# The out projection of a hybrid encoder block as seven quarter products, with sums of its weights kept in HBM

## The chip, the core and the metric

The kernel runs on one core of a Trainium2 chip. A core has TensorE (PE: matrix products into PSUM), VectorE (DVE), ScalarE (ACT), GpSimd (POOL) and SyncE (SP), which issues most DMAs; all work out of an on-chip memory (SBUF) and PSUM. The metric is the device time of one launch in microseconds (us), lower is better, as the median of several runs.

## The reference

One block over 1024 tokens of 1024 channels, with 16 meta tokens ahead:

```python
h = h + hybrid_mixer(rmsnorm(h, norm_mix), w_in, ..., w_out)
h = h + squared_relu_mlp(rmsnorm(h, norm_ffn), w_ff1, w_ff2)
return rmsnorm(h, norm_final)[:, N_META:]
```

The mixer projects the normed tokens with w_in, makes a pooled branch y_a (trailing means over 2, 4, 8 and 16 positions, a small mix per group, then w_pool_out) and a gated linear attention branch y_b (chunks of 64, then w_gla_out), and merges them:

```python
m = jax.nn.sigmoid(ga) * y_a + jax.nn.sigmoid(gb) * y_b
return jnp.einsum('bld,de->ble', m, w_out)
```

The change is in this last product (1024 x 1024 times 1024 x 1024), called the out projection here, and in what stands directly before and behind it.

## The kernel before

All operands are f32. A product in full precision is made of three: each operand is split into a high part (ScalarE copies it to fp32r) and a low part (VectorE or GpSimd subtracts the copy), and mm3 (L253) issues high x high, high x low and low x high for each 128 x 128 tile of the stationary side and 512 columns of the moving side. So every operand costs a ScalarE copy and a subtraction before TensorE can use it, and 512 columns over a depth of 512 (four tiles) cost 12 matmuls.

The program is one list of steps in the order of TensorE's work, which is written out by hand. Where `in_order` is set for ScalarE and VectorE, these engines take their instructions in the order in which the code issues them; where `any_order` is set, a scheduler places them. GpSimd's order and SyncE's are in the listings below the change. Each engine runs its own list strictly in order: an instruction that waits holds up all that stand behind it on that engine.

The stages, in the order of time: the norm and the projections with w_in; at 240 to 320 us the pooling, where `a_block` projects one group of 128 channels, `mean_block` (L921) makes its trailing means on VectorE, and `mix_block` (L938) multiplies them with w_pool_mix (mw, whose low half is made on GpSimd in L902); the attention; then `yb_block` (L1152), which multiplies the attention's output with w_gla_out, gates it, adds the pooled branch and leaves the merged m, split, in MH (high) and ML (low), one pair for each half of 512 tokens. For the second half of the tokens (h = 1) this runs at about 460 to 488 us.

Out projection before (488.5 to 581 us): `load_wo` (L1518) splits w_out into S["wo"], in pieces of 256 rows by 512 columns; `out_tile(t, ch)` (L1545) multiplies token tile t (128 tokens) with one half ch of the columns: 24 matmuls into one PSUM bank, then VectorE adds the bank to x, which lies in acc (L1559). All eight tiles go with ch = 0 first, then in ORDER with ch = 1. After ch = 1 the row of a tile is complete, and `layer_norm` makes its norm: Square with a running sum on ScalarE (L245), Ln and Exp (L221, L223), four small VectorE instructions, and the scaling (`scaled`, L249) into u2. `turn_tile` (L1567) then transposes the normed tile on TensorE (8 matmuls with the identity, L1577) two tiles later, and makes from it the operands of the first MLP product FF1, which already runs as seven products of sums of quarters: for tiles 0 to 3 the split, and a raw copy of the transposed tile (L1582); for tiles 4 to 7 differences with those raw copies, split into S["wo"][0] (L1599).

Behind that: `ff_weights` (L1642) primes FF1's weights, `ff_room` (L1659) splits one more operand of FF1, called P4 (L1664, L1665), and makes place for h, the hidden values of the MLP. `ff_result` (L1687) forms h, its sums S1, S2, S5, S6, S7, and stores them (`keep`); `ff2_open` (L1713) opens the operands fx of the second MLP product FF2, which reads the stored sums back.

Of the kernel before, what the change touches and what calls it, by code (L numbers as in the profile page):

```python
# [115 lines left out]
def kernel(  # L116
# [52 lines left out]
    pm_dram = dp.tile([2, 2, P, 4, HALF], F32, name="pm_dram")  # L169
    hf_dram = [dp.tile([NPAIR, P, HALF], F32, name=f"hf{m}_dram") for m in range(7)]  # L170
# [66 lines left out]
    def layer_norm(xt, u):  # L237

        scaled(xt, u, inv_rms(xt, u))

    def inv_rms(xt, u):
        rows = xt.shape[0]
        ss = ln_stat[ln_n[0] % 4][:rows]
        ln_n[0] += 1
        act.activation(u, xt, ACT.Square, accum_out=ss)  # L245
        return inv_sqrt(ss, 1, 1.0 / D)

# [21 lines left out]

    def split(a):  # L270

        hi, lo = next_slot()
        if len(a.shape) == 3:
            hi, lo = quad(hi), quad(lo)
        act.activation(hi, a, ACT.Copy)  # L275
        dve.tensor_tensor(lo, a, f32(hi), ALU.subtract)  # L276
        return hi, lo
# [611 lines left out]
    def pool_open():  # L889
# [13 lines left out]
        raw.lend(left.push("raw2", [P, D], F32))  # L903

# [94 lines left out]
    v_ = lambda i: step(one, lambda: load_vw(i))  # L999
    for f, i in (  # L1000
        (a_, 3), (p_, 3), (a_, 2), (m_, 3), (p_, 2), (a_, 1), (m_, 2), (p_, 1), (a_, 0), (m_, 1), (v_, 1), (p_, 0),
    ):
        f(i)
# [127 lines left out]
    def early_gates():  # L1131
# [7 lines left out]
        fetch_wo(0, 0, S["raw3"])  # L1139
# [12 lines left out]
    def yb_block(n, h):  # L1152
        j = YB[h][n]

        def fn(*wbs):
# [6 lines left out]
            for e in range(2):  # L1162
# [20 lines left out]
                if h and e and n == 1:  # L1183
                    load_wo(0, 1)()
                if not h:
                    dve.tensor_tensor(gl, b, gl, ALU.mult)
                dve.tensor_tensor(gl, gl, ml, ALU.add)
# [297 lines left out]
    def merge_open():  # L1485
# [4 lines left out]
        S["wo"] = [left.push("wo0", [P, 2, KT, HALF], F32R)]  # L1490
        S["left_acc"] = left.mark()
        S["acc"] = left.push("acc", [P, 8, D], F32)
# [4 lines left out]
        fetch_wo(0, 1, S["acc"][:, 5])  # L1497
# [8 lines left out]
    fetched = {}  # L1506

    def fetch_wo(ch, kk, at=None):

        c, rows = slice(ch * HALF, (ch + 1) * HALF), w_out[kk * 256 : (kk + 1) * 256]  # L1510
        ap = rows[:, c].rearrange("(k p) c -> p k c", p=P)
        if at is None:
            at = raw.load(ap, D)
        else:
            nc.sync.dma_start(at.rearrange("p (k c) -> p k c", k=2), ap)
        fetched[ch, kk] = at.rearrange("p (k c) -> p k c", k=2)

    def load_wo(ch, kk):  # L1518
        def fn():
            if (ch, kk) not in fetched:  # L1520
                fetch_wo(ch, kk)
            wo, r = S["wo"][ch][:, :, 2 * kk : 2 * kk + 2], fetched.pop((ch, kk))
            act.activation(wo[:, 0], r, ACT.Copy)
            pending.append(lambda: dve.tensor_tensor(wo[:, 1], r, f32(wo[:, 0]), ALU.subtract))
            if ch:
                late()

        return fn

    step(one, merge_open)  # L1530
    def wo1_open():
        any_order("order")
        raw.back()
        right.pop_to(0)
        buffer("u2", 2, D)
        S["u2p"] = right.push("u2p", [P, 2, HALF], F32)
        S["rawx0"] = right.push("rawx0", [P, D], F32)
        raw.lend(S["rawx0"])
        S["right_ff"] = right.mark()
        S["wo"].append(right.push("wo1", [P, 2, KT, HALF], F32R))  # L1540


    ORDER = (0, 4, 1, 5, 2, 3, 6, 7)

    def out_tile(t, ch):  # L1545
        def fn():
            half, at = t // 4, (t % 4) * P
            wo = S["wo"][ch]
            b, n = bank("mm"), ORDER.index(t)
            for j in range(2):  # L1550
                if ch and j and n > 1:
                    turn_tile(ORDER[n - 2])
                mm3(
                    b, KT // 2, lambda i: (MH[half][:, 4 * j + i, at : at + P], ML[half][:, 4 * j + i, at : at + P]),
                    lambda i: (wo[:, 0, 4 * j + i], wo[:, 1, 4 * j + i]), first=j == 0, last=j == 1,
                )
            a = S["acc"][:, t, ch * HALF : (ch + 1) * HALF]
            with tc.high_priority(offset=AHEAD) if ch else nullcontext():
                dve.tensor_tensor(a, b, a, ALU.add)  # L1559
                if ch:  # L1560
                    layer_norm(S["acc"][:, t], S["u2"][:, n % 2])
            if ch:
                nc.sync.dma_start(h_dram[t], S["acc"][:, t])

        return fn

    def turn_tile(t, tags=("ms",), later=None):  # L1567
# [25 lines left out]
        def differences():  # L1593
            dve.tensor_tensor(lo, b[1], t1, ALU.subtract)
            dve.tensor_tensor(b12, b[1], b12, ALU.subtract)
            dve.tensor_tensor(hi, hi, lo, ALU.subtract)
            for n, a in enumerate((lo, b12)):
                fh, fl = (S["wo"][0][:, k, 4 * n : 4 * n + 4, cols] for k in range(2))
                act.activation(fh, a, ACT.Copy)  # L1599
                dve.tensor_tensor(fl, a, f32(fh), ALU.subtract)  # L1600
# [5 lines left out]

    for n, j in enumerate(YB[1]):
        if n != 1:
            step(one, load_wo(0, n))
# [4 lines left out]
        if n < 2:  # L1614
            step(one, lambda kk=n + 2: fetch_wo(0, kk, S["acc"][:, 4 + kk]))
    step(one, load_gB)
    step(one, wo1_open)
    step(one, lambda: x_again(0))
    step(one, lambda: x_again(1))
    for t in range(8):  # L1620
        if t < 6:
# [296 lines left out]
```

## Time and profile before

| | |
|---|---|
| median of 3 runs | 1202.03 us (1201.92 to 1202.49) |
| span of the profiled execution | 1200.9 us, 1.1 below the median of the runs |
| TensorE busy | 1189.0 us, 99%, 6810 matmuls |
| VectorE, ScalarE, GpSimd busy | 873.0, 624.7 and 64.8 us |
| out projection | first matmul at 488.52 us; FF1's first matmul at about 581 |

The profiled execution's own time is taken as its span. Times in rows of the timeline are from the start of the span. A matmul's listed duration runs on beneath the next one, so the distance between starts is what counts. In a group's row the last part is the idle time of that engine just before the instructions, and what ended it. "b_mm", "b_x" and "b_ms" are PSUM banks; "th", "tl" are high and low halves of an operand on the token side, "w1h", "w1l" of a weight.

### The profile page before, as it was taken

Reading aid. Unit: us, or ns where it says so; the run is one execution under the profiler, and the core shown is the slowest. Engines: PE = TensorE matmul, PEld = TensorE weight load, DVE = VectorE, ACT = ScalarE, POOL = GpSimd, SP = SyncE. Lnnn points to the kernel's source line nnn. Section 1 sums busy time; section 2 is a strip of 40 time slices with the busy share of each in tenths; the row PEclk is TensorE's granted clock in tenths of the full one; section 3 lists DMA queues with packets and bytes.
Section 4 is the critical chain, followed back from the end, with each engine's and each line's share of the span. In section 5 each row is a group of like instructions: output and inputs, shape, how many; then the busy total and the mean of one; then the engine's idle time right before and its main releaser. Section 6 shows DMA issues by size and latency. Waiting matters only on the chain.

```text
span 1200.9 us, 18410 instructions
## 1 busy us (share of the span) xinstructions
PE 1189.0 (99%) x6810; PEld 995.0 (83%) x6810; DVE 873.0 (73%) x1436; ACT 624.7 (52%) x1120; POOL 64.8 (5%) x102
## 2 busy tenths in 40 slices
PE   9999999999999999999999999999999999999997
PEld 8888888898998887888888888888888888888885
DVE  7886677666667888637986767767675887887686
ACT  7677567745446433215654545545454444445554
POOL 2200000000103235000000000000000000000000
PEclk9999999999999999999999999999999999999999
DMA  8243433535107676821264444445389963333532
GB/s 259 36 115 116 126 92 99 156 116 161 50 20 265 196 245 196 323 69 77 88 202 132 158 149 160 148 157 164 125 283 332 330 220 97 97 97 97 167 97 88
DMA packets 143722, 183.29 MB, mean 153 GB/s; under 512 B 10328, under 2 KB 80752, under 8 KB 143120
## 3 DMA queue, kind: packets, MB, share of 16 engines
q1 hardware_dynamic: 141648, 176.55, 45.8%
q0 software_dynamic: 1824, 5.31, 1.5%
q8 instruction: 53, 0.87, 0.3%
q14 instruction: 37, 0.30, 0.1%
q10 hardware_dynamic: 160, 0.27, 0.1%
HBM read 124.41 MB, written 57.67 MB: 152 GB/s over the span
## 4 chain that ended last, share of the span: by engine, by line
PE 91%; DVE 3%; DMA 3%; ACT 1%; issue 1%; SPq 0%; POOL 0%; DVEq 0%; ACTq 0%
PE b_mm L257 10%; PE b_mm L259 10%; PE b_mm L258 10%; PE b_ms L259 10%; PE b_ms L258 10%; PE b_ms L257 10%; PE b_x L257 8%; PE b_x L258 8%; PE b_x L259 8%; PE b_sc L1278 1%; PE b_mx L257 1%; DMA ma_dram<-o 1%; PE b_mx L259 1%; PE b_mx L258 1%; DMA o<-ma_dram 1%; DMA t<-gb_dram 1%
## 5 line engine op out<-in xcount | busy, mean ns | idle before, releaser
L257 PE MATMUL b_mm<-th,w1h 128*128 128x512 f32 (+1 forms) x308 | 115.4, 375 | 0.3 <-DVE c L847 0.3
L259 PE MATMUL b_mm<-th,w1l 128*128 128x512 f32 (+1 forms) x308 | 114.2, 371 | 0.0
L258 PE MATMUL b_mm<-tl,w1h 128*128 128x512 f32 (+1 forms) x308 | 114.1, 371 | 0.0
L257 PE MATMUL b_x<-th,w1h 128*128 128x512 f32 (+1 forms) x264 | 100.2, 380 | 0.0
L258 PE MATMUL b_x<-tl,w1h 128*128 128x512 f32 (+1 forms) x264 | 100.1, 379 | 0.0
L259 PE MATMUL b_x<-th,w1l 128*128 128x512 f32 (+1 forms) x264 | 99.7, 378 | 0.0
L275 ACT ACTIVATE w1h<-raw 128x512 fp32r<-128x512 f32 x98 | 60.7, 620 | 27.9 <-PE b_ms L258 13.6
L275 ACT ACTIVATE w1h<-fs 128x512 fp32r<-128x512 f32 x78 | 49.0, 630 | 48.3 <-PE b_ms L258 34.4
L276 DVE TENSOR_TENSOR w1l<-raw,w1h 128x512 fp32r<-128x512 f32 x98 | 67.1, 686 | 8.3 <-ACT w1h L275 8.3
L257 PEld LDWEIGHTS b_mm<-th,w1h 128*128 128x128 f32 x308 | 57.8, 188 | 11.0 <-issue 0.7
L259 PEld LDWEIGHTS b_mm<-th,w1l 128*128 128x128 f32 x308 | 57.8, 188 | 10.1
L258 PEld LDWEIGHTS b_mm<-tl,w1h 128*128 128x128 f32 x308 | 57.9, 188 | 9.6
L276 DVE TENSOR_TENSOR w1l<-fs,w1h 128x512 fp32r<-128x512 f32 x78 | 53.4, 687 | 16.6 <-ACT w1h L275 16.6
L275 ACT ACTIVATE w1h<-bt 128x512 fp32r<-128x512 f32 x44 | 27.8, 632 | 66.8 <-issue 62.7
L259 PEld LDWEIGHTS b_x<-th,w1l 128*128 128x128 f32 x264 | 49.7, 188 | 9.6
L257 PEld LDWEIGHTS b_x<-th,w1h 128*128 128x128 f32 x264 | 49.6, 188 | 9.5
L258 PEld LDWEIGHTS b_x<-tl,w1h 128*128 128x128 f32 x264 | 49.6, 188 | 9.2
L1753 DVE TENSOR_TENSOR bt<-w,w 128x512 f32<-128x512 f32 x80 | 54.8, 685 | 0.6 <-DMA w<-in_w_ff_dram 0.6
L275 ACT ACTIVATE fxh<-bt 128x512 fp32r<-128x512 f32 x36 | 22.8, 632 | 55.7 <-issue 49.8
L275 ACT ACTIVATE w1h<-rawx 128x512 fp32r<-128x512 f32 x44 | 27.4, 628 | 44.6 <-PE b_x L258 18.6
L259 PE MATMUL b_ms<-wo,w1l 128*128 128x512 f32 x128 | 49.9, 390 | 0.0
L257 PE MATMUL b_ms<-wo,w1h 128*128 128x512 f32 x128 | 49.8, 389 | 0.0
(455 smaller groups left out, 3342.3 us busy)
## 6 DMA issues: line engine op xcount, KB each, us to landing
hf_dram<-h SPq DMA_DIRECT2D x112, 256.0 KB, 2.1
raw<-hf_dram SPq DMA_DIRECT2D x112, 256.0 KB, 2.6
w<-in_w_ff_dram SPq DMA_DIRECT2D x64, 256.0 KB, 4.6
raw<-in_w_in_dram SPq DMA_DIRECT2D x22, 512.0 KB, 4.6
raw<-in_w_ff_dram SPq DMA_DIRECT2D x16, 512.0 KB, 4.1
rawx<-in_w_ff_dram SPq DMA_DIRECT2D x16, 512.0 KB, 4.2
rawx<-in_w_in_dram SPq DMA_DIRECT2D x10, 512.0 KB, 4.3
xs<-in_x_dram SPq DMA_DIRECT2D x8, 512.0 KB, 4.9
```

What stands on the lines that cost most here:

```text
L257: pe.matmul(ps, ah, bh, start=first and i == 0, stop=False, skip_group_check=more)
L258: pe.matmul(ps, ah, bl, start=False, stop=False, skip_group_check=more)
L259: pe.matmul(ps, al, bh, start=False, stop=last and i == n - 1, skip_group_check=more)
L275: act.activation(hi, a, ACT.Copy)
L276: dve.tensor_tensor(lo, a, f32(hi), ALU.subtract)
L1278: pe.matmul(b[to, e, j], kk[r, s], qq[r, s], start=True, stop=True, tile_position=(e * CH, u * CH))
L1753: dve.tensor_tensor(bt, w, S["w2"][q[3:]][:, i], ALU.add if q[2] == "+" else ALU.subtract)
```

## The change

With tokens and channels each cut in halves, the projection is a product of 2 x 2 quarters. Instead of eight quarter products it makes seven, of sums of quarters on both sides (P1 and P2, a product with T2, one with T1, and three called third, seventh and fourth by their functions), and adds the results.

- `wo_sums`, on GpSimd during the pooling stage: the four weight sums T1 to T4 are made from w_out's quarters in two halves, and stored to HBM (wt_dram). It is issued behind the first `mean_block`.
- In `yb_block` for the second half of the tokens, the first four channel tiles are no longer split: only their plain sum is kept (in "sums"), and all eight are written there.
- `merge_open` has GpSimd make plain sums of high and low halves of the first token half (`top`); `out_projection` makes from these the token sums (VectorE and GpSimd), splits them into MH and ML, and issues the seven products, one token tile of 12 matmuls at a time.
- The products third, seventh and fourth are interleaved with rows and turns: third(t) completes row t; seventh(t) opens a bank, fourth(t) adds to it and completes row 4 + t. Rows now complete in another order, ORDER = (0, 1, 2, 4, 3, 5, 6, 7).
- The row's norm is made by `first_rms` (one small VectorE instruction less), in two pieces: `row` issues the Square, Ln and Exp, `normed` the smalls and the scaling.
- In `turn_tile` the raw copies and part of the later differences and their low halves go to GpSimd, as do the low halves of FF1's first four weight quarters.
- P4's operand now lies in wx, which is also the place of T4, read by the product fourth. F takes S["wo"][0]'s part. h moves into acc (16 halves) and the first row of u2 (2 halves), which lies where FF2's fx is opened later.

The core of the diff:

```diff
+    def wo_sums():
+        b11, b12, b22, b21 = (S["tsum"][:, n] for n in range(4))
+        for q in range(2):
+            for t, j, k in ((b11, 0, 0), (b12, 0, 1), (b22, 1, 1), (b21, 1, 0)):
+                pool.dma_start(pieces(t), wo_part(j, k, q))
+            for n, (to, a, b) in enumerate(((b11, b12, b11), (b12, b22, b12), (b22, b22, b11), (b21, b21, b22))):
+                pool.tensor_tensor(to, a, b, ALU.subtract)
+                pool.dma_start(wt_dram[n, q], to)
...
-        (a_, 3), (p_, 3), (a_, 2), (m_, 3), (p_, 2), (a_, 1), (m_, 2), (p_, 1), (a_, 0), (m_, 1), (v_, 1), (p_, 0),
+        (a_, 3), (p_, 3), (o_, 0), (a_, 2), (m_, 3), (p_, 2), (a_, 1), (m_, 2), (p_, 1), (a_, 0), (m_, 1), (v_, 1), (p_, 0),
...
+        for t in range(4):
+            b = bank("ms")
+            product(b, form[1, 0], "T1", t)
+            dve.tensor_tensor(w[:, t], b, u[:, t], ALU.add)
+            by_tile(t)
+            add(t, right_of, w[:, t], pool)
+            add(4 + t, right_of, w[:, t], pool)
+            add(4 + t, left_of, u[:, t], pool)
...
+        third(0)
+        sides("T4", 0)
+        normed(0)
+        third(1)
+        rounded("T4", 1, pool)()
+        normed(1)
...
+        seventh(0)
+        turn_tile(0)
+        third(2)
+        turn_tile(1)
+        normed(2)
+        fourth(0)
+        seventh(1)
+        normed(4)
+        turn_tile(2)
+        third(3)
...
+        turn_tile(4, later=later)
+        normed(3)
+        later.pop()()
+        fourth(1)
+        ff_weights()
+        seventh(2)
+        normed(5)
+        turn_tile(3)
+        seventh(3)
+        turn_tile(5, later=later)
+        fourth(2)
+        later.pop()()
+        normed(6)
+        fourth(3)
...
-                act.activation(raw_copy, b[j], ACT.Copy)
-                split_from_psum(MH[0][:, k, cols], ML[0][:, k, cols], b[j])
+                h, l = MH[0][:, k, cols], ML[0][:, k, cols]
+                split_from_psum(h, l, b[j])
+                pool.tensor_tensor(raw_copy, f32(h), f32(l), ALU.add)
...
-        ff_quarters.x["P4"] = tuple(right.push("t4" + k, [P, 4, HALF], F32R) for k in "hl")
+        ff_quarters.x["P4"] = S["wx"][:, 0], S["wx"][:, 1]
...
-        S["h"] = left.push("h", [P, 2, 9, HALF], F32)
+        units = [S["acc"][:, t, c] for t in range(8) for c in halves()] + [S["u2"][:, 0, c] for c in halves()]
+        S["h"] = units[:9], units[9:]
```

How this stands in the engines' lists, at three places. First GpSimd in the pooling stage, before (tl is an operand of the attention that follows; w1l the low half of a weight):

```order
L562 MEMSET lr 80x512
L902 TENSOR_TENSOR mw<-raw_116,mw 128x512
L88 TENSOR_TENSOR w1l<-raw_116,w1h 128x256 x4
L562 MEMSET lr 80x512
L1081 DMA tl_144<-pm_dram 128x2048
```

and after, from the same place (tsum holds the quarters of w_out, then their sums):

```order
L911 DMA tsum<-in_w_out_dram 128x2x512 x4
L913 TENSOR_TENSOR tsum<-tsum 128x1024
L554 MEMSET lr 80x512
L914 DMA wt_dram<-tsum 128x1024
L894 TENSOR_TENSOR mw<-raw_117,mw 128x512
L913 TENSOR_TENSOR tsum<-tsum 128x1024
L914 DMA wt_dram<-tsum 128x1024
```

The split of mw now has four loads, a subtraction and a store in front of it; seven more subtractions and stores follow.

Second, VectorE where the first finished row is normed: before, row 0 (acc is x plus the projection, small the statistics, u_5067 the normed row):

```order
L1559 TENSOR_TENSOR acc<-b_mm,acc 128x512 [waits PE_49]
L222 TENSOR_SCALAR small<-small 128x1 [waits Activation_49]
L225 SCALAR_TENSOR_TENSOR small<-small 128x1 [waits DVE_49,Activation_49]
L229 TENSOR_SCALAR small<-small 128x1 [waits DVE_49]
L230 TENSOR_TENSOR small<-small 128x1 [waits DVE_49]
L249 SCALAR_TENSOR_TENSOR u_5067<-acc,small,gB 128x1024 [waits DVE_49]
```

and after (wx takes T4):

```order
L1632 TENSOR_TENSOR acc<-b_mm,acc 128x512 [waits PE_49,Pool_49]
L1555 TENSOR_TENSOR wx<-raw_117,wx 128x1024 [waits DMAHW2_49,Activation_49]
L623 TENSOR_SCALAR small<-small 128x1
L625 SCALAR_TENSOR_TENSOR small<-small 128x1 [waits DVE_49]
L626 SCALAR_TENSOR_TENSOR small<-small 128x1 [waits DVE_49]
L239 SCALAR_TENSOR_TENSOR u_5117<-acc,small,gB 128x1024 [waits DVE_49]
```

The low half of T4's first part now stands between the addition and the statistics, and waits for ScalarE and a DMA.

Third, ScalarE at row 6, after (wx now takes P4's operand, F the differences of a turn; L618 is the Square, L620 and L621 are Ln and Exp):

```order
L618 ACTIVATE u_5117,small<-acc 128x1024 [waits DMAHW3_49,DVE_49]
L1863 ACTIVATE wx<-acc 128x4x128 [waits PE_49,Pool_49]
L620 ACTIVATE small<-small 128x1 [waits Activation_49]
L1863 ACTIVATE wx<-acc 128x4x128 [waits Pool_49]
L621 ACTIVATE small<-small 128x1 [waits Activation_49]
L1802 ACTIVATE F<-acc 128x4x128 [waits DVE_49] x2
```

Before, the same row had Square, Ln and Exp one behind the other (L245, L221, L223), and P4's copies had a place of their own. Now the first copy into wx, which waits for TensorE and GpSimd, stands between the Square and the logarithm.

More of the change, by code (lines that the diff above doesn't have):

```diff
@@ L1534, in wo1_open, with out_projection @@
+    def out_projection():
         right.pop_to(0)
-        buffer("u2", 2, D)
+        u, w = (left.push("o" + n, [P, 4, HALF], F32) for n in "uw")
         S["u2p"] = right.push("u2p", [P, 2, HALF], F32)
         S["rawx0"] = right.push("rawx0", [P, D], F32)
-        raw.lend(S["rawx0"])
+        S["u2"] = right.push("u2", [P, 2, D], F32)
         S["right_ff"] = right.mark()
[L1540 to L1565, printed above, removed]
@@ new lines, in normed, with third, seventh, fourth @@
+        def normed(t):
+            scaled(acc[:, t], S["u2"][:, ORDER.index(t) % 2], next(rms.pop(t)))
+        def third(t):
+            b = bank("mm")
+            product(b, form[0, 1], "B22", t)
+            add(t, right_of, b)
+            row(t)
+        def seventh(t):
+            b = held[t] = bank("x")
+            product(b, form[1, 0], "T3", t, last=False)
+            add(4 + t, right_of, b)
+        def fourth(t):
+            b = held.pop(t)
+            product(b, form[1, 1], "T4", t, first=False)
+            add(4 + t, left_of, b)
+            row(4 + t)
```

259 lines of the change are left out of this document (192 added, 67 removed).

## The prediction

> **What bounds the kernel now.** I read the page first: the busy shares, the slices, the chain that ended last.
>
> ```profile
> span 1200.9 us, 18410 instructions
> PE 1189.0 (99%) x6810; PEld 995.0 (83%) x6810; DVE 873.0 (73%) x1436; ACT 624.7 (52%) x1120; POOL 64.8 (5%) x102
> POOL 2200000000103235000000000000000000000000
> PE 91%; DVE 3%; DMA 3%; ACT 1%; issue 1%; SPq 0%; POOL 0%; DVEq 0%; ACTq 0%
> ```
>
> TensorE is busy 99% of the span and carries 91% of the chain, so taking matmuls away shortens the kernel as long as no other engine takes over the wait. GpSimd (POOL) is nearly empty and has nothing to do after slice 15, that is after some 480 us. Next I looked at the stretches around the out projection (columns: stretch, its length, then busy us and instructions of PE, PEld, DVE, ACT, POOL, then clock, DMA share, GB/s).
>
> ```profile
> 440.00:475.00 35.00, 34.14 (x236) 27.14 (x235) 27.70 (x44) 13.37 (x22) 24.15 (x28) 1.00 0.65 212
> 475.00:500.00 25.00, 24.95 (x111) 20.34 (x110) 19.57 (x28) 8.38 (x12) 0.00 (x0) 1.00 0.81 273
> 500.00:520.00 20.00, 20.00 (x90) 16.57 (x89) 8.86 (x11) 6.30 (x8) 0.00 (x0) 1.00 0.83 290
> 520.00:540.00 20.00, 20.00 (x90) 16.57 (x89) 3.89 (x7) 1.47 (x4) 0.00 (x0) 1.00 0.03 10
> 540.00:560.00 20.00, 20.00 (x102) 16.80 (x101) 14.23 (x31) 10.85 (x25) 0.00 (x0) 1.00 0.24 96
> 560.00:582.00 22.00, 22.00 (x110) 18.44 (x109) 18.03 (x36) 13.55 (x29) 0.00 (x0) 1.00 0.18 73
> ```
>
> From 500 to 582 TensorE has no gap at the full granted clock (1.00). There is no wait in the projection that the change could remove; all it can win is matmuls, and every wait that it makes is new. VectorE (DVE) has room only between 500 and 540: 12.75 of 40 us.
>
> **What is saved.** The rate and the chain that finishes a row, from the timeline inside the projection:
>
> ```profile
> 537.59 0.39 PE L259 MATMUL b_mm<-wo,tl 128*128 128x512 f32 x1
> 538.02 0.69 DVE L1559 TENSOR_TENSOR acc<-b_mm,acc 128x512 f32<-128x512 f32 x1 [4.75 <-PE b_mm L259]
> 538.75 1.06 ACT L245 ACTIVATE u<-acc 128x1024 f32<-128x1024 f32 x1 [18.50 <-DVE acc L1559]
> 540.25 0.20 ACT L223 ACTIVATE small<-small 128x1 f32<-128x1 f32 x1
> 541.12 1.28 DVE L249 SCALAR_TENSOR_TENSOR u<-acc,small,gB 128x1024 f32<-128x1024 f32 x1
> 541.22 0.39 PE L257 MATMUL b_x<-wo,th 128*128 128x512 f32 x1
> 545.75 0.39 PE L259 MATMUL b_x<-wo,tl 128*128 128x512 f32 x1
> ```
>
> From 541.22 to 545.75 stand 20 steps: 4.53 / 20 = 0.2265 us per matmul. Before, 16 half rows take 24 matmuls each, 384; after, 7 products of 4 token tiles take 12 each, 336. So 48 x 0.2265 = **-10.9 us**. This is certain; the rest is what comes between.
>
> **Edit 1: the sums of w_out while pooling.** GpSimd gets 8 subtractions of 128x1024, 8 loads of 512 KB and 8 stores. No row shows GpSimd at that size; the nearest is 128x512:
>
> ```profile
> L902 POOL TENSOR_TENSOR mw<-raw,mw 128x512 fp32r<-128x512 f32 x1 | 1.3, 1287 | 9.0 <-DMA gb_dram<-o 9.0
> 255.05 3.77 DVE L928 TENSOR_TENSOR s<-s 128x1036 f32<-128x1036 f32 x3
> 260.77 1.29 DVE L934 TENSOR_TENSOR ph<-s,ph 128x512 fp32r<-128x512 f32 x2 [0.70 <-ACT ph L933]
> 262.90 0.39 PE L257 MATMUL b_ms<-ph,mw 128*128 128x512 f32 x1
> ```
>
> Twice 1.287 is 2.57 us, so 8 x 2.57 = 20.6 us of GpSimd (an estimate from L902). As work that is free: the engine idles there. Two things are not. The split of mw (L902, now L894) is queued behind the first four loads and the first subtraction, but it has from 247 to 262.9 before TensorE asks for it; I cost that at nothing (if the loads land in more than some 12 us, mixing waits for the excess). And VectorE's pooling chain, instructions with two SBUF inputs back to back, ends at 260.77 + 1.29 = 262.06, only 0.84 us before TensorE reads ph. What GpSimd does to such instructions shows in the last bursts of before, 440 to 475 us (first two rows: GpSimd; then VectorE's groups of that window):
>
> ```profile
> 444.53 1.43 POOL L1194 TENSOR_TENSOR tl<-t,th 128x256 fp32r<-128x256 f32 x2 [1.29 <-ACT th L1190]
> 461.87 5.58 POOL L1194 TENSOR_TENSOR tl<-t,th 128x256 fp32r<-128x256 f32 x6
> L1187 DVE TENSOR_TENSOR t<-t,o 128x512 f32<-128x512 f32 x9 | 8.6, 959 | 1.3 <-DMA o<-ma_dram 1.0
> L1443 DVE TENSOR_TENSOR yg<-mix,yg 128x512 fp32r<-128x512 f32 x3 | 3.1, 1051 | 0.0
> L1192 DVE TENSOR_TENSOR tl<-t,th 128x512 fp32r<-128x512 f32 x1 | 1.1, 1144 | 0.1
> L1186 DVE TENSOR_TENSOR t<-b_mm,t 128x512 f32<-128x512 f32 x5 | 3.4, 684 | 0.7 <-DMA t<-gb_dram 0.7
> ```
>
> L1186, one input in PSUM, takes 684 ns. The same size with both inputs in SBUF takes 959, 1051 and 1144 on the mean while GpSimd works: a loss of 9 x 0.275 + 3 x 0.367 + 0.46 = 4.0 us. GpSimd pays too: six instructions in 5.58 us where two undisturbed take 1.43 (4.29 for six). Of its 24.15 us in that window 28 x 0.715 = 20.0 are work. So VectorE loses 4.0 / 20.0 = **0.20 us per us of GpSimd work**, and GpSimd as much again (4.15 / 20.0). For the pooling: 20.6 x 0.20 = 4.1, less the 0.84 of slack (the first of four such stretches takes the most): **+3.0**, ends 0 (GpSimd works where VectorE waits for ScalarE) and +8 (each of three GpSimd instructions of 2.57 us stands once in front of the chain).
>
> [...]
>
> **Edit 2: token sums, splits and raw copies on GpSimd in the projection.** There GpSimd gets 50 instructions of 128x512 (8 half sums, 8 differences, 12 additions, 2 tile splits, 8 raw copies, 4 + 4 of the later differences, 4 splits of FF1's weights) and one of 128x1024: 50 x 1.287 + 2.57 = 66.9 us in the 107 - 11 = 96 us from 475. At the rate above VectorE loses 66.9 x 0.20 = 13.4 us. Thirty of the 51 come before the first finished row, where VectorE had 27 us of room; the other half comes where VectorE was 32.3 of 42 us busy and every row waits for it. I take half: **+6.6**, ends 0 and 13.4 + 13.9 of GpSimd's own = 27.
>
> **Edit 3: the new order of rows.** Before, a row had 36 matmuls (8.2 us) between its addition and its turn. The chain from addition to u ready takes 541.12 + 1.28 - 538.02 = 4.4 us, so it was covered. After, the turn of row 0 stands 24 matmuls behind, 24 x 0.2265 = 5.44 us, and the addition starts 538.02 - 537.59 - 0.23 = 0.20 into it: 5.24 us are left. Between the addition and the scaling of row 0 on VectorE now stands the split of T4's first quarter, and ScalarE makes its high half after row 0's exponential: 540.25 + 0.20 - 538.02 = 2.43, then ScalarE 1.06, VectorE 1.22 (row below), smalls and scaling 541.12 + 1.28 - 540.45 = 1.95: 6.66 us.
>
> ```profile
> 491.75 1.23 DVE L1524 TENSOR_TENSOR wo<-acc,wo 128x1024 fp32r<-128x1024 f32 x1 [0.26 <-ACT wo L1523]
> 878.85 0.63 ACT L275 ACTIVATE fxh<-raw 128x512 fp32r<-128x512 f32 x1
> 892.30 0.69 DVE L1706 TENSOR_TENSOR h<-h 128x512 f32<-128x512 f32 x1
> 893.65 0.39 PE L257 MATMUL b_x<-fxh 128*128 128x512 f32 x1
> hf_dram<-h SPq DMA_DIRECT2D x112, 256.0 KB, 2.1
> ```
>
> Turn 0 waits **1.4**. Row 6 is the other case: its Square is followed on ScalarE by the copy of P4's operand into wx, and that waits for TensorE to finish the last T4 product (which reads wx) and for GpSimd, whose queue has four weight splits ahead; Ln and Exp of row 6 are behind it. From the end of that product: 0.4 to the end of the last matmul, copies 2 x 0.63 with Ln and Exp 0.5 between, VectorE's smalls 0.63, one split of F that stands ahead 0.69, the scaling 1.28, semaphores some 0.4: 5.2 us, against 12 matmuls, 2.7 us, that TensorE has in between: **+2.5**. The other joints (turns 1 to 5 and 7, the fourth product of tile 0 on T4's split on GpSimd, the seventh product of tile 3 on a bank whose addition is queued behind turn 4) each lie between 0 and 1.4; I take 0.5 each for eight, **+4.0**.
>
> **Edit 4: h in acc and u2.** The two halves for S6 and S7 of odd pairs now lie over u2, and FF2's fx tiles over these; a copy into fx must wait until the last S6 is stored. Before, the fx copies ran from 878.85. Now: S6 ends 892.30 + 0.69 = 892.99, its store lands 2.1 later, 895.1, ScalarE's copy 0.63, VectorE's low half 0.69: 896.4, where TensorE wants it at 893.65 + 0.23 = 893.9. **+2.6** for the first operand, 0.5 more at most for the second. Nothing else can be put in front of it in TensorE's order. All else (fewer splits in yb, loads of x moved, one queue on SyncE that was at most 0.83 of the DMA engines busy) I cost at nothing: TensorE's order doesn't ask for them earlier; if SyncE's queue did run late, its price would be that of one 512 KB landing, some us, within the range.
>
> **The sum.** -10.9 + 3.0 + 6.6 + 1.4 + 2.5 + 4.0 + 2.6 = +9.2. Execution shown: 1200.9; its median of runs is 1202.03, 1.1 above; so 1202.0 + 9.2 = **1211**. The low end of all terms together, -10.9 + 2.6 + 1.4 = -6.9, gives 1195; with everything at its upper end it would be -10.9 + 8 + 27 + 15 + 3 = +42, which cannot all add up, since one wait gives the other engines time.
>
> **Rivals.**
> *The saving goes through.* For: GpSimd idle after 480, VectorE 12.75 of 40 us busy where the sums are made; the contention then falls on idle time, and each wait of TensorE gives the row chains back what they lost, so that few of the joints in series wait. Against: the row chain after third(0) is longer than its cover by the working above. It decides at 5.24 us: if T4's split comes before the addition or after the scaling, 4.4 fits and the later rows follow. Then only FF2's 2.6 and some 2 to 3 of joints remain: -10.9 + 2.6 + 2.3 = -6.0, **1196**. Chance 0.35.
> *Full exclusion.* If any overlapping pair is served one after the other, VectorE loses what GpSimd uses wherever both want to run. In the projection that is 13.4 of VectorE and 13.9 of GpSimd's own, in the row chains about half of the sum, 13.6 for 6.6, and the pooling pays 8 for 3.0: +21, **1223**. For: L1443 and L1192 lost over half their length. Against: in before the mean loss per VectorE instruction was 0.3 to 0.46, not a whole GpSimd instruction. Chance 0.15. [...]
> *Gains and waits cancel*, within 0.2% (2.4 us, about what a measurement of this kernel can tell from no change): needs the joints at 1 and the contention at 1: 0.06. That the change doesn't do what it says cannot be: the 48 matmuls are gone from TensorE's order.
>
> **How the numbers follow.** Forecast 0.44 (own range 1205 to 1218), full exclusion 0.15, no change 0.06, saving through 0.35. Faster: 0.35 of the first rival; same 0.06; slower 0.44 + 0.15 = 0.59. The range goes from 1195 (first rival with nothing else waiting) to 1224 (full exclusion): what is left out is about 0.1 below and 0.1 above.
>
> **What would show it.** TensorE 48 matmuls fewer, and in the projection its idle time: a gap of 1 to 2 us before the turn of row 0, of 2 to 3 before that of row 6, and of 2.6 before FF2's first matmul on fx; 128x512 splits and sums of VectorE with two SBUF inputs at 0.9 to 1.2 us while GpSimd works; a gap of some us before the first mixing product near 263. The forecast is wrong if the projection shows TensorE without gaps (then 1196), or if GpSimd's 128x512 takes far from 1.29 us.

## The result, and the profile after

The changed kernel takes 1239.37 us (median of 4 runs, 1237.67 to 1240.84), the kernel before 1201.97. The ratio is 1.0311, 95% interval 1.0296 to 1.0326: slower by 37 us, above the range of the prediction. The page of its profiled execution:

```profile
span 1239.1 us, 18487 instructions
PE 1198.7 (97%) x6762; PEld 999.0 (81%) x6762; DVE 926.5 (75%) x1437; ACT 634.0 (51%) x1128; POOL 180.2 (15%) x177
POOL 2100000171103247664410000000000000000000
PEclk9999999998999999998899999999999999999999
PE 86%; DVE 7%; ACT 3%; issue 1%; DMA 1%; POOL 1%; SPq 0%; DVEq 0%; POOLq 0%; ACTq 0%
```

The 48 matmuls are gone (6762 for 6810), yet TensorE is busy 9.7 us longer, and the row of its clock has three slices at 8, where before all stood at 9. So time went in two ways: TensorE waits, and it runs slower. The stretches show both (the third column from the end is the granted clock):

```profile
240.00:285.00 45.00, 39.14 (x227) 34.15 (x226) 34.49 (x22) 16.23 (x29) 29.79 (x24) 0.94 0.82 273
540.00:560.00 20.00, 15.85 (x71) 12.86 (x70) 13.04 (x15) 4.50 (x8) 16.22 (x12) 0.99 0.50 174
560.00:580.00 20.00, 16.53 (x72) 13.53 (x71) 15.18 (x21) 8.70 (x19) 8.14 (x6) 0.84 0.28 105
600.00:620.00 20.00, 15.12 (x65) 12.40 (x64) 13.67 (x24) 10.02 (x22) 5.32 (x4) 0.83 0.21 79
900.00:940.00 40.00, 35.99 (x146) 28.82 (x145) 23.52 (x37) 19.09 (x33) 0.00 (x0) 0.91 0.79 263
```

The timeline of TensorE names the waits. Its six longest (in brackets the idle time before the row, and what ended it):

```profile
265.16 0.50 PE L247 MATMUL b_ms<-ph,mw 128*128 128x512 f32 x1 [2.14 <-ACT ph L946]
283.67 0.79 PE L247 MATMUL b_ms<-ph,mw 128*128 128x512 f32 x1 [3.50 <-ACT ph L946]
559.75 1.94 PE L1779 MATMUL b_ms<-ident,u 128*128 128x128 f32 x8 [4.15 <-DVE u L239]
568.52 1.10 PE L1779 MATMUL b_ms<-ident,u 128*128 128x128 f32 x8 [3.47 <-DVE u L239]
608.87 1.94 PE L1779 MATMUL b_ms<-ident,u 128*128 128x128 f32 x8 [4.88 <-DVE u L239]
928.74 0.80 PE L247 MATMUL b_x<-fxh 128*128 128x512 f32 x1 [4.00 <-DMA raw<-hf_dram]
```

They are two mixing products of the pooling, the turns of rows 0, 1 and 6, and FF2's first product on fx. With the shorter ones (1.14 and 1.57 at the end of yb, 0.63 and 2.01 before the turn of row 3 and the last seventh product, 1.47 and 0.37 in FF1, 0.22 in the pooling) they make 29.6 us.

And at the end of each of these six, or a few us behind it, the clock stood at half: 267 to 269, 283 to 289, 560 to 562, 571 to 573, 608 to 614 and 930 to 934 us ran at 0.50. Two-microsecond stretches behind the wait that ends at 283.67:

```profile
283.00:285.00 2.00, 1.33 (x3) 0.80 (x4) 1.29 (x2) 2.00 (x4) 0.00 (x0) 0.50 0.64 262
287.00:289.00 2.00, 2.00 (x11) 2.00 (x11) 2.00 (x4) 1.38 (x4) 0.00 (x0) 0.50 0.56 91
289.00:291.00 2.00, 2.00 (x15) 2.00 (x15) 1.94 (x3) 0.00 (x0) 0.00 (x0) 0.80 1.03 347
291.00:293.00 2.00, 2.00 (x19) 2.00 (x18) 1.86 (x2) 0.39 (x1) 0.00 (x0) 1.00 1.07 332
```

Some 6 us at clock 0.50 for a wait of 3.50: about 3 us of work time lost on top. Over the whole span the mean granted clock is 0.982, before 0.998: 0.018 x 1239.1 = 22.3 us lost against 0.002 x 1200.9 = 2.4, so the clock costs 19.9 us. The account closes: 29.6 of waits, of which the kernel before has 0.9 too, + 19.9 of clock - 10.9 of matmuls = 37.7, and the spans differ by 38.2.

By stages, from the starts of the same products in both timelines:

| start of | before | after | lost in the stage ahead |
|---|---|---|---|
| the attention's scores | 312.06 | 323.11 | 11.1 |
| the out projection | 488.52 | 503.76 | 4.2 |
| FF1 | 581.36 | 601.11 | 4.5 (15.4 against the 10.9 saved) |
| FF2 | 888.21 | 919.14 | 11.2 (the turns of rows 6 and 7 lie here) |
| FF2's first product on fx | 893.65 | 928.74 | 4.2, and 3 behind it at low clock |

### The profile page after: what moved, and what is told of

Read it like the earlier page. It is cut to its first block, busy times and chain, and to the rows that moved or that the text cites. A ratio compares the mean times of both kernels' runs of the same rounds, so it can differ in the third digit from the quotient of the medians.

```text
span 1239.1 us, 18487 instructions
## 1 busy us (share of the span) xinstructions
PE 1198.7 (97%) x6762; PEld 999.0 (81%) x6762; DVE 926.5 (75%) x1437; ACT 634.0 (51%) x1128; POOL 180.2 (15%) x177
## 4 chain that ended last, share of the span: by engine, by line
PE 86%; DVE 7%; ACT 3%; issue 1%; DMA 1%; POOL 1%; SPq 0%; DVEq 0%; POOLq 0%; ACTq 0%
PE b_ms L248 10%; PE b_ms L247 10%; PE b_ms L249 10%; PE b_mm L247 9%; PE b_mm L249 9%; PE b_mm L248 9%; PE b_x L247 7%; PE b_x L248 7%; PE b_x L249 7%; DVE s L941 2%; PE b_mx L247 1%; PE b_sc L1299 1%; PE b_mx L249 1%; PE b_mx L248 1%; DVE u L239 1%
## 5 line engine op out<-in xcount | busy, mean ns | idle before, releaser
L247 PE MATMUL b_ms<-F,w1h 128*128 128x512 f32 x128 | 50.0, 391 | 0.0
L248 PE MATMUL b_ms<-F,w1h 128*128 128x512 f32 x128 | 49.9, 390 | 0.0
L249 PE MATMUL b_ms<-F,w1l 128*128 128x512 f32 x128 | 49.8, 389 | 0.0
```

Of the source, the lines that this page charges most:

```text
L247: pe.matmul(ps, ah, bh, start=first and i == 0, stop=False, skip_group_check=more)
L248: pe.matmul(ps, ah, bl, start=False, stop=False, skip_group_check=more)
L249: pe.matmul(ps, al, bh, start=False, stop=last and i == n - 1, skip_group_check=more)
```

## Experiments

Theory A: a GpSimd instruction that reads SBUF keeps VectorE's instructions with two SBUF inputs out for its whole length; the chains on VectorE get late, TensorE waits, and its clock halves. Rivals: B, in the pooling the loads and stores of the sums, or the place of mw's split behind them; C, in the projection VectorE's load and the order of its list.

### What holds the pooling

Left out in one kernel: the eight subtractions. In a second, each is replaced by two memsets of the same tile.

```diff
-                pool.tensor_tensor(to, a, b, ALU.subtract)
+                pool.memset(to, 0.0)
+                pool.memset(to, 0.0)
```

> GpSimd's eight subtractions while pooling are left out (the loads and stores stay, so the weight sums are wrong). Theory A (a GpSimd instruction that reads SBUF keeps VectorE's two-input instructions out for its whole length; the gaps that follow also halve TensorE's clock): the pooling chain returns to 1.2 us per instruction, the gaps of 2.1, 0.2 and 3.5 us before the mixing products go, the attention's first product comes at about 312 us instead of 323.1, and the time falls by 11 to about 1228. Rival B (the loads and stores, or the place of mw's split behind them, hold up the mixing): gaps and time stay, 1239.

> Each of the eight subtractions is replaced by two memsets of the same tile, so that GpSimd is busy about as long but reads nothing (the sums are wrong). Theory A in its form that only reads of GpSimd contend: as without the subtractions, about 1228, pooling chain at 1.2 us per instruction. Theory A2 (any GpSimd work on SBUF keeps VectorE out): gaps and time stay near 1239. Rival B: 1239 too, with the pooling chain undisturbed.

Measured: without subtractions 1233.9 us (ratio 1.0270, 1.0240 to 1.0300), with memsets 1231.8 (1.0253, 1.0217 to 1.0288; its two runs, 1230.0 and 1233.6, lie 3.6 apart). Both miss the expected 1228 by some us, so the stage itself has to decide. VectorE's pooling chain in the changed kernel, with a GpSimd row beside it:

```profile
253.78 2.44 POOL L913 TENSOR_TENSOR tsum<-tsum 128x1024 f32<-128x1024 f32 x1
253.88 3.44 DVE L941 TENSOR_TENSOR s<-a 128x1038 f32<-128x1038 f32 x1
257.35 5.84 DVE L941 TENSOR_TENSOR s<-s 128x1036 f32<-128x1036 f32 x3
279.63 3.26 DVE L944 SCALAR_TENSOR_TENSOR s<-s,a 128x1024 f32<-128x1024 f32 x1
```

and with the memsets, GpSimd just as busy at that place:

```profile
252.55 1.87 POOL L913 MEMSET tsum<- 128x1024 f32 x2
253.50 1.23 DVE L942 TENSOR_TENSOR s<-a 128x1038 f32<-128x1038 f32 x1
254.76 3.77 DVE L942 TENSOR_TENSOR s<-s 128x1036 f32<-128x1036 f32 x3
```

3.44 us for an instruction of 1.23 is its own length and 2.2 us of GpSimd's 2.4. With memsets the chain is back at its old times, the scores start at 311.72, before at 312.06, and the stage has its 11 us back. So in the changed kernel it is GpSimd's reading, not its work or its DMAs. In the kernel without subtractions VectorE's chain is back too, but a wait of 2.7 us before the second mixing product came up (scores at 318.67, so only 4.4 of the 11 are back): there the split of vw stood before the high half of ph on ScalarE and waited 6.1 us for its load, while GpSimd's loads and stores, no longer held up by arithmetic, came in a row. That it was these DMAs is argued, not shown.

The sums were also to run elsewhere, behind the last mean block:

```diff
-        (a_, 3), (p_, 3), (o_, 0), (a_, 2), (m_, 3), (p_, 2), ... (v_, 1), (p_, 0),
+        (a_, 3), (p_, 3), (a_, 2), (m_, 3), (p_, 2), ... (v_, 1), (p_, 0), (o_, 0),
```

> The step with the weight sums on GpSimd is issued behind the last mean block instead of behind the first; all is computed. Theory of the exclusion: the pooling's gaps (5.9 us and the low clock behind them, 11 in all) go, and come back only where VectorE's two-input instructions of the attention's start have no room; VectorE is busy 47 of 75 us there: about 1229. If the sums cost the same wherever they run: 1239.

This told nothing: 1239.4 us (1.0313, 1.0297 to 1.0328), but the scheduler put the sums where they had been (the third one of them at 253.63 in place of 253.78), since only the place in the code was moved.

### GpSimd in the projection

First all of its instructions there went to VectorE (the half sums to the start of the projection), then the pooling's sums as well.

```diff
-            add(t, right_of, w[:, t], pool)
+            add(t, right_of, w[:, t])
-                pool.tensor_tensor(raw_copy, f32(h), f32(l), ALU.add)
+                dve.tensor_tensor(raw_copy, f32(h), f32(l), ALU.add)
... (and so for all 51)
```

> All that GpSimd does in the projection, the turns and FF1's first splits goes to VectorE (the first half sums then stand at the start of the projection); the pooling stays as changed. Theory A: a 128x512 instruction on GpSimd stands 1.29 us in VectorE's way, on VectorE itself 0.60, so although VectorE gets some 31 us more to do, the gaps before the turns of rows 0, 1 and 6 shrink to half, about 1225. Rival C (VectorE's load and the order of its list are what is late, not the exclusion): VectorE, full between 500 and 540, gets later by up to 31 us, and the time rises to 1245 or more.

> As the one before, and the eight subtractions while pooling on VectorE as well. Theory A: both gains add, 1239 - 11 (less some 9 us of VectorE work in pooling, of which it had 15 idle) - 14: about 1214. Rival C: above 1240.

Measured 1235.7 (1.0285, 1.0255 to 1.0315) and 1235.5 (1.0284, 1.0254 to 1.0313). Neither theory's number: the exclusion's gain is eaten by VectorE's load. In the first half of the projection VectorE is then busy 52 of 55 us, and the gap before the turn of row 0 is 3.84 us with no GpSimd at all:

```profile
497.00:552.00 55.00, 52.43 (x231) 42.68 (x229) 52.21 (x66) 21.17 (x28) 0.00 (x0) 1.00 0.57 200
```

In the second of these the sums stand in VectorE's list between the steps of the pooling, and the chain waits 5.6 us for a load of theirs: the first mixing product waits 6.00 us.

So VectorE's list had to be kept and only GpSimd's reading taken away: memsets of the same outputs, which leave out what GpSimd computes.

```diff
-            pool.tensor_tensor(top(k), f32(MH[0][:, k]), f32(ML[0][:, k]), ALU.add)
+            pool.memset(top(k), 0.0)
... (and so for all 51)
```

> Every instruction of GpSimd in the projection, the turns and FF1's first splits is replaced by a memset of the same output, so GpSimd keeps its place but reads nothing, and waits for no input (the results are wrong); VectorE's and ScalarE's lists stay as changed. Theory of the exclusion: what is left in the stage are the waits of the order alone, by my own working 1.4 at row 0, 2.5 at row 6 and about 0.5 at the others, instead of 4.15, 4.88, 3.47, 2.01 and 1.5; with the low clock that follows each, the time falls by 12 to 17, to about 1224. Theory of the order alone: the gaps before the turns of rows 0, 1 and 6 stay within 1 us of the changed kernel's, and the time above 1234.

1218.6 us (1.0138, 1.0122 to 1.0153): 20.8 us less than the changed kernel, more than the 12 to 17 expected. A memset also waits for no input, and is shorter (0.5 us instead of 1.3). To separate that, the same outputs were written as differences of two halves of a constant: reads, but no input to wait for (the first eight half sums stay as changed, with their reads and their waits).

```diff
-                pool.tensor_tensor(raw_copy, f32(h), f32(l), ALU.add)
+                pool.tensor_tensor(raw_copy, quad(gB[:, :HALF]), quad(gB[:, HALF:]), ALU.subtract)
... (and so for 43)
```

> As with the memsets in the projection, but GpSimd's instructions (all but the first eight half sums, which stay as changed) subtract two halves of a constant in SBUF, so they read as much as the changed kernel's and still wait for no input (results wrong). Exclusion by reads: the time goes back up from 1218.6 to 1232 or more, and VectorE's two-input instructions are stretched again. Rival (the memsets helped because GpSimd no longer waited for inputs, so its results were never late): the time stays within 4 us of 1218.6.

1233.0 us (1.0265, 1.0249 to 1.0280): 14.4 of the 20.8 us come back, and 6.4 don't. The starts of the same products show where (lost against the kernel before, us; FF1 has the turns of rows 6 and 7):

| kernel | pooling | end of yb | projection | FF1 | fx | behind it |
|---|---|---|---|---|---|---|
| changed | 11.1 | 4.2 | 4.5 | 11.2 | 4.2 | 3.3 |
| memsets | 8.8 | -0.3 | -4.7 | 4.9 | 4.3 | 2.8 |
| reads of a constant | 10.0 | 4.6 | 3.7 | 4.9 | 3.9 | 3.1 |

The 4.9 us at the end of yb come back with the half sums, which are whole again; in the changed kernel VectorE's L88 takes 2.27 us beside them (494.70), with memsets 1.22. The 8.4 in the projection come back with the reads alone. The 6.3 of FF1 stay away although the reads are back: they are what GpSimd's lateness cost, shown below for row 6. The pooling's code is the same in all three, and its loss still differs by 1 to 2 us; differences of that size in one stage say nothing.

Row 0's norm on VectorE shows the mechanism in three kernels. As changed (L625 and L626 are 128x1, L239 the scaling; the first two rows are what GpSimd runs beside them):

```profile
552.57 3.52 POOL L1632 TENSOR_TENSOR acc<-ow,acc 128x512 f32<-128x512 f32 x2
556.05 1.26 POOL L1623 TENSOR_TENSOR tl<-sums,th 128x512 fp32r<-128x512 f32 x1
554.87 0.14 DVE L623 TENSOR_SCALAR small<-small 128x1 f32<-128x1 f32 x1
555.05 1.05 DVE L625 SCALAR_TENSOR_TENSOR small<-small 128x1 f32<-128x1 f32 x1
556.14 1.18 DVE L626 SCALAR_TENSOR_TENSOR small<-small 128x1 f32<-128x1 f32 x1
557.36 2.25 DVE L239 SCALAR_TENSOR_TENSOR u<-acc,small,gB 128x1024 f32<-128x1024 f32 x1
```

with memsets (GpSimd's last one ahead of this ends at 543.8; the last two rows are the turns of rows 0 and 6):

```profile
548.20 0.22 DVE L628 SCALAR_TENSOR_TENSOR small<-small 128x1 f32<-128x1 f32 x1
548.45 0.16 DVE L629 SCALAR_TENSOR_TENSOR small<-small 128x1 f32<-128x1 f32 x1
548.65 1.28 DVE L239 SCALAR_TENSOR_TENSOR u<-acc,small,gB 128x1024 f32<-128x1024 f32 x1
550.08 1.06 PE L1791 MATMUL b_ms<-ident,u 128*128 128x128 f32 x8 [1.22 <-DVE u L239]
590.55 1.57 PE L1791 MATMUL b_ms<-ident,u 128*128 128x128 f32 x8 [2.52 <-DVE u L239]
```

and with reads of a constant:

```profile
554.88 2.24 POOL L1627 TENSOR_TENSOR tl<-gB 128x512 fp32r<-128x512 f32 x1
556.11 1.04 DVE L628 SCALAR_TENSOR_TENSOR small<-small 128x1 f32<-128x1 f32 x1
557.18 1.18 DVE L629 SCALAR_TENSOR_TENSOR small<-small 128x1 f32<-128x1 f32 x1
558.40 2.25 DVE L239 SCALAR_TENSOR_TENSOR u<-acc,small,gB 128x1024 f32<-128x1024 f32 x1
560.79 1.94 PE L1791 MATMUL b_ms<-ident,u 128*128 128x128 f32 x8 [5.03 <-DVE u L239]
605.00 1.26 PE L1791 MATMUL b_ms<-ident,u 128*128 128x128 f32 x8 [2.52 <-DVE u L239]
```

The two instructions of one column with two SBUF inputs ended only with the GpSimd instruction beside them: as changed, L625 ends at 556.10 and L626 at 557.32, GpSimd's at 556.09 and 557.31. L623, with one, takes 0.14 beside GpSimd's 3.52, and 0.15 with memsets. With GpSimd out of the way, row 0's chain from addition to scaling takes 6.5 us, its turn waits 1.22, and row 6's 2.52.

Row 6 is another case. It waits 2.52 with reads of a constant too, where GpSimd's last instruction ends at 590.8, ahead of that norm. As changed, ScalarE's second copy of P4's operand, which stands ahead of row 6's exponential, waits for GpSimd's sum:

```profile
602.26 1.80 POOL L1799 TENSOR_TENSOR acc<-acc 128x512 f32<-128x512 f32 x1
604.10 0.63 ACT L1863 ACTIVATE wx<-acc 128x512 fp32r<-128x512 f32 x1 [1.72 <-POOL acc L1799]
```

So of the 2.4 us that row 6 waits above 2.52, GpSimd's lateness is the larger part, and the rest is exclusion (L625 at 606.16 takes 1.05 us instead of 0.22).

The half of GpSimd's work that lies in the turns was undone by itself (raw copies on ScalarE, the rest on VectorE):

```diff
-                pool.tensor_tensor(raw_copy, f32(h), f32(l), ALU.add)
+                act.activation(raw_copy, b[j], ACT.Copy)
-            pool.tensor_tensor(hi, hi, lo, ALU.subtract)
+            dve.tensor_tensor(hi, hi, lo, ALU.subtract)
-        low_by[0] = pool
```

> GpSimd's part of the turns is undone: raw copies on ScalarE from PSUM, differences, T4's second split and FF1's first low halves on VectorE, as in the kernel before; sums and additions ahead of the first row stay on GpSimd. All is computed. Exclusion: the gap before the turn of row 6 and FF1's of 1.5 go below 3 in sum instead of 6.4, row 0's stays, since the additions on GpSimd are still running; about 1230. Rival (VectorE's load is what is late): VectorE gets 8 us more, the gaps grow, 1239 or above.

1237.7 us (1.0300, 1.0283 to 1.0317), 1.7 less than the changed kernel and nearer to the rival's 1239 than to 1230. Row 0 still waits 4.45 us, as expected. Row 6 waits only 1.81, no longer held by GpSimd, but row 5 now waits 4.78, VectorE having more to do. Undone on VectorE's account, this half of the work gains next to nothing.

### The order of the lists

```diff
         third(0)
-        sides("T4", 0)
         normed(0)
         third(1)
-        rounded("T4", 1, pool)()
         normed(1)
+        sides("T4", 0)
+        rounded("T4", 1, pool)()
```

> T4's two splits are issued behind the norms of rows 0 and 1 instead of between addition and norm; nothing else changes. Theory of the order (the split stands in row 0's chain on ScalarE and VectorE): the gap of 4.15 us before the turn of row 0 loses about 2.3 us, and the low clock behind it gets shorter, together 4 us, to about 1235. Theory of the exclusion alone (what holds the chain are GpSimd's instructions): the gap stays within 1 us, the time within 2 us of 1239.

and for P4:

```diff
                 later[1]()
-                any_order("order")
             next(run)
         ff_room()
+        any_order("order")
```

> The scheduler's freedom is given back only behind the copies of P4's operand, so that they stand behind rows 6 and 7 on ScalarE and VectorE instead of between Square and logarithm of row 6. Theory of the order: the gap of 4.88 us before the turn of row 6 loses 2 to 3 us, and the time falls by 4 to 5, to about 1235. Theory of the exclusion alone: the gap stays above 4 us, 1238.

1237.3 us (1.0299, 1.0282 to 1.0315) and 1238.7 (1.0306, 1.0291 to 1.0322): 2.1 and 0.7 less, too little for the times to decide. Both gaps shrink as the order says, and the wait moves on. With T4's splits later (rows 0 and 1):

```profile
557.62 1.06 PE L1779 MATMUL b_ms<-ident,u 128*128 128x128 f32 x8 [0.99 <-DVE u L239]
565.79 1.59 PE L1779 MATMUL b_ms<-ident,u 128*128 128x128 f32 x8 [4.36 <-DVE u L239]
```

With P4's copies later (row 6, then FF1's product on F):

```profile
606.85 1.94 PE L1779 MATMUL b_ms<-ident,u 128*128 128x128 f32 x8 [3.05 <-DVE u L239]
628.09 0.50 PE L247 MATMUL b_ms<-F,w1h 128*128 128x512 f32 x1 [2.98 <-ACT w1h L267]
```

### FF2's opening and the clock

The first row here is the last store out of u2; ScalarE's copy into fx, which lies over the same place, waits for it (changed kernel):

```profile
923.35 0.32 SPq L1884 DMA_DIRECT2D hf_dram<-u  x1
```

```profile
927.54 0.63 ACT L267 ACTIVATE fxh<-raw 128x512 fp32r<-128x512 f32 x1 [0.70 <-DMA hf_dram<-u]
```

```diff
-        S["h"] = units[:9], units[9:]
+        S["h"] = units[:9], units[9:14] + units[16:] + units[14:16]
```

> The two halves of u2 that lie under FF2's fx hold S1 and S5 of odd pairs instead of S6 and S7; they are stored some 3 to 5 us earlier. The gap of 4.00 us before FF2's first matmul on fx falls to 0.7 or less. Theory with the clock (a gap of this length is followed by about 6.5 us at half clock): the time falls by 3.3 of gap and 3.3 of clock, to about 1232.5. Without it: by 3.3, to 1236.

1235.6 us (1.0273, 1.0253 to 1.0293), 3.8 less, nearer to the figure without the clock. The stage itself shows both: the gap is 1.09 instead of 4.00, the stretch of 905 to 945 us runs at clock 1.00 instead of 0.91, and of the time lost at fx and behind it 2.9 and 2.5 us go.

```profile
925.87 0.50 PE L247 MATMUL b_x<-fxh 128*128 128x512 f32 x1 [1.09 <-DMA hf_dram<-acc]
```

The clock by itself: matmuls that nobody reads, put into four gaps.

```diff
+            if j == 0 and t in (0, 1):
+                for _ in range(14 if t == 0 else 11):
+                    pe.matmul(place, slot["T3"][0][:, 0, :P], slot["T3"][0][:, 1], start=True, stop=True)
... (28 of 128 columns for row 6, 14 before FF2's first product on fx)
```

> Matmuls whose result nobody reads are put in front of the turns of rows 0, 1 and 6 (14, 11 and 28 smaller ones) and of FF2's first fx product (14), so that they run inside the gaps of 4.15, 3.47, 4.88 and 4.00 us. Theory with the clock: the idle time that is left is too short to lower the clock, TensorE goes on at full speed behind each gap, and the time falls by some 2.5 to 3.3 us for each of the four, 10 to 13 in all, to about 1228, although no wait is shorter. Without it (the low clock has another cause, or costs nothing because the following products are early): the time stays at 1239 or rises by what of the extra matmuls outlasts the gaps.

1232.3 us (1.0254, 1.0239 to 1.0270): 7.1 us faster by adding work to the engine that bounds the kernel. The changed kernel's two stretches, then those of this one:

```profile
530.00:640.00 110.00, 93.02 (x398) 75.24 (x398) 86.19 (x119) 49.54 (x95) 52.40 (x35) 0.91 0.31 109
905.00:945.00 40.00, 35.99 (x146) 28.82 (x145) 22.92 (x36) 18.32 (x32) 0.00 (x0) 0.91 0.85 280
```

```profile
530.00:640.00 110.00, 99.56 (x470) 81.18 (x469) 88.75 (x127) 52.22 (x100) 53.41 (x35) 0.98 0.34 117
905.00:945.00 40.00, 39.04 (x170) 31.41 (x170) 23.88 (x38) 17.64 (x32) 0.00 (x0) 1.00 0.93 309
```

The gain is less than the 10 to 13 expected, and some 2 us of it lie in the pooling, where nothing was changed (9.0 us lost there instead of 11.1). Behind rows 0 and 1 and behind fx it works: 3.5 us in the projection and 2.5 behind fx. Row 6 still waits 2.08 us in spite of its fillers, and 604.3 to 607.7 us run at clock 0.50.

### All together

> All suspected causes taken away at once: memsets in place of GpSimd's reads while pooling and in the projection (results wrong), T4's splits behind the norms of rows 0 and 1, P4's copies behind rows 6 and 7, S1 and S5 in u2. If these are the causes, the 48 matmuls show: 1202 - 10.9 + some 5 for the small gaps that I don't touch (bank of the seventh product of tile 3, end of the second branch) = about 1196, faster than before. If the time stays above 1206, a cause that I haven't named holds more than 10 us.

1206.8 us (1.0035, 1.0025 to 1.0045): 32.6 of the 37.4 us are gone, but it is 11 above the expected 1196, so the causes named don't hold everything. The profile has 12.7 us of waits in it (2.83 before a mixing product whose chain had waited for a load of vw, 0.2 to 1.4 at ten joints of projection and FF1, 1.4 at fx), before 0.9; with 1.2 of clock and the 10.9 saved that is 2 above the kernel before, and the spans differ by 5.4. Most of the rest lies in the joints too. The listed wait is shorter than what the starts lose, since the matmul ahead runs on beneath it: the wait listed as 1.10 lies between starts at 598.73 and 600.22, 1.49 us where 0.23 is usual, so it costs 1.26. By an estimate of 0.16 us for each of some 13 waits, 2 of the 3 us are these; 1 stays open.

The versions that leave nothing out, first with the mends of order, S1 and S5 in u2 and the fillers, then with the turns undone in place of P4's copies moved:

> A version that computes all, with every single mend together: sums behind the last mean block, T4's splits and P4's copies moved behind the norms, S1 and S5 in u2, and matmuls without a reader inside the gaps that remain. If the gains add: 11 + 2 + 1 + 4 + 5 = 23 off 1239, about 1216; the exclusion in the projection is left in it, so I don't expect it below 1202.

> The same with T4's splits behind the norms of rows 0 and 1, S1 and S5 in u2, and matmuls without a reader in the gaps. All is computed. If the mends add: 1230 - 4 - 7 + what the fillers outlast, about 1221; the pooling's 11 us and the exclusion ahead of the first row stay in it, so it isn't expected to beat the kernel before.

1229.4 us (1.0231, 1.0211 to 1.0250) where 1216 was expected; the sums of the pooling were not moved in it, as above, and the pooling loses 9.5 us. And 1231.1 (1.0245, 1.0229 to 1.0260) where 1221 was expected, in a sum that began at 1230 for a kernel that took 1237.7. No version that leaves nothing out beats the kernel before; the exclusion ahead of the first row and in the pooling is in both.

## Why the prediction was wrong

**What bounds the kernel, and the saving:** right. 48 matmuls fewer, and no wait in the projection that could be removed.

**The sum:** this is the step that failed. It added waits to matmuls at full rate and had no term for the clock: it read a clock of 1.00 from 500 to 582 us in the kernel before, where TensorE has no gap, and put what new waits do to the clock at nothing, without a reason. 19.9 of the 48 us that were lost against the saving are low clock. The terms for waits were too small as well: they come to 20.1 us, 28.7 were measured. Filling four gaps showed the clock directly (0.91 became 0.98 in one stretch and 1.00 in the other). A wait of 2.14 us (265.16) was enough: 267 to 269 us ran at 0.50. So were shorter ones: behind waits of 1.14 and 1.57 (494.72, 497.02) 498 to 500 us ran at 0.50, and behind one of 1.47 (626.81) 628 to 630. But it did not follow each time. Around a wait of 2.01 us before the last seventh product, 588 to 598 us ran at 0.83 in the changed kernel; with the turns undone that wait was 2.44, and the ten steps behind it, from 590.13 to 592.42, took 0.22 to 0.24 us each, the full rate. With all suspected causes off, the steps behind a wait of 2.83 before a mixing product (298.23) were 0.22 to 0.24 us too, from 299.29 on. What decides it, no run shows.

**Edit 1, pooling, +3.0 (ends 0 and 8):** mis-sized, 11.1 measured: 5.9 of waits and the rest clock. GpSimd's work was right, 19.8 us of subtractions for 20.6. The rate was not: beside them L941 and L944 lost 2.2, 2.1, 1.9, 4.2 and 2.0 us against the kernel with memsets, 12.4 in all, or 0.62 us per us instead of 0.20. The rate was a mean over thirteen instructions of one stretch, and it isn't shown how many of them met GpSimd; here the chain is two-input instructions back to back, and six times one of them waited for the rest of an instruction of 2.4 us. The bound of 8, which counted whole instructions, was the better reading of the waits.

**Edit 2, the projection, +6.6 (ends 0 and 27):** mis-sized. Taking GpSimd's reads and input waits away gave 20.8 us with the clock: by the stages some 5 at the end of yb, 8 to 9 in the projection, 6 at rows 6 and 7, the rest scatter in the pooling. The first two are exclusion, the third is mostly GpSimd's lateness. The exclusion shows in single instructions: beside GpSimd's reads L626 took 1.18 us instead of 0.16 at row 0, beside memsets the first step of the pooling chain took 1.23 instead of 3.44, and L623 at row 0, with one SBUF input, took 0.14 beside the reads. The rival of full exclusion had this mechanism, at 1223; with the clock it would have been near the result.

**Edit 3, the order:** right in its sizes once GpSimd's reads and its waits for inputs are away: 1.22 for row 0 (forecast 1.4), 2.52 for row 6 (2.5), and 1.39, 0.65, 1.44, 0.55 and 0.38 at the others, 4.4 (4.0). That the small ones add up so closely is luck: 0.5 was taken for each of eight, and five came, between 0.38 and 1.44. What failed was to add contention as an average beside it: at row 0 it fell onto just this chain and made 4.15 of it. At row 6 the working named the wait for GpSimd's queue but counted only from TensorE's product; that wait and some exclusion made 4.88 of it.

**Edit 4, h in u2, +2.6:** right in mechanism, 4.00 of wait and about 3 of clock. The store was issued at 923.35 and ended ScalarE's wait at about 927.5, some 4 us against the median of 2.1.

**The rival of the saving going through** failed at its point of decision as worked out: row 0's chain was longer than 5.24 us, 6.5 with memsets and 9.3 as changed.

## What to carry to other kernels

An idle engine isn't free to give work to: ask what its instructions read and which engine waits for them, and price a VectorE instruction with two SBUF inputs beside a reading GpSimd at its own length plus the rest of GpSimd's, even a small one: here 3.44 us for 1.23 in the pooling, and 1.18 for 0.16 at row 0. A result that an idle engine makes late costs too, here most of 6.3 us at rows 6 and 7. When TensorE is busy 99% at full clock, price new waits with the low clock that can follow them: here 29.6 us of waits brought 19.9 of it, and with everything on VectorE 31.0 of waits brought about 14 (clock 0.987). Look for the chain that each new wait delays before counting matmuls saved.

## What was not expected of the hardware

A wait of 2.14 us on TensorE was followed by about 3 us at half clock, one of 3.50 us by about 6. VectorE instructions of 128x1 with two SBUF inputs took 1.05 and 1.18 us instead of 0.22 and 0.16. Matmuls without a reader in four gaps made the kernel 7.1 us faster.
